# Gram products and attention scores that alternate between the two heads of a pair

## The chip, the cores and the metric

One core of one Trainium2 chip runs the whole program. The metric is the device time of one execution in microseconds (us); less is better. The core has five engines with queues of their own: PE (TensorE, matrix products into PSUM), DVE (VectorE), ACT (ScalarE), POOL (GpSimd) and SP (SyncE, which here issues most transfers). PEld stands for PE's loads of the stationary operand.

## The reference, cut to what matters

Two layers run over 512 tokens (256 of context, then 256 of a latent grid) with 1024 channels. Each layer has a mixer and a gated MLP. The mixer has three branches: a bidirectional RWKV-7 recurrence, a gated linear recurrence and a neighbourhood attention, the first and the last with 16 heads of 64 channels. The change concerns two places. In the recurrence, whose step is

```
sa = jnp.einsum('bhvk,bhk->bhv', S, -kk_t)
S = (S * w_t[:, :, None, :] + sa[..., None] * (kk_t * a_t)[:, :, None, :]
     + v_t[..., None] * k_t[:, :, None, :])
return S, jnp.einsum('bhvk,bhk->bhv', S, r_t)
```

the kernel works by chunks of 64 tokens and needs, for each chunk, head and direction, the products of all keys with all decayed queries of the chunk (the Gram products). In the attention it needs the scores

```
s_loc = jnp.einsum('bhnqd,bhnkd->bhnqk', qb, kb).astype(jnp.float32) * scale + bias.astype(jnp.float32)
s_ctx = jnp.einsum('bhnqd,bhld->bhnql', qpb, k_ctx).astype(jnp.float32) * scale
prob = jax.nn.softmax(jnp.concatenate([s_loc, s_ctx], axis=-1), axis=-1).astype(v.dtype)
```

and, in layer 0 alone, plain attention among the context tokens. Layer 1 puts out latent tokens only.

## The kernel before, in words

Channels lie on the 128 partitions, tokens on the free axis. A channel tile of 128 is a pair of heads: head 0 on partitions 0 to 63, head 1 on 64 to 127. A layer's mixers (`mixers`) loop over 8 pairs. For each pair a string of letters (`order` in `CFG`) says in which order its parts are traced: `1` and `2` prepare a pair for the recurrence (`rw_key`, `rw_prep`), `g` is `rw_gram`, `v` `rw_rows`, `i` and `I` the inverse of the chunks' triangular systems (`rw_inv`, 31 dependent steps on DVE at lines 664 and 666, and `rw_inv2`), `T` the recurrence over the 8 chunks (`rw_seq`), `X`, `Y`, `a`, `b`, `S` the linear recurrence, `Q`, `A` and `P` the attention, `G` and `N` the merge gates. Most of PE's time goes to the projections: `proj` calls `mm3` (lines 246 to 248), which multiplies weights in two parts (`wh`, `wl`) with activations in two parts. `wload` makes these parts: a transfer on SP's queue, `wh` on ACT (line 225), `wl` on DVE or POOL (line 228).

The order on each engine is fixed when the program is built. A list scheduler takes, whenever an engine is free in its forecast, the instruction of highest priority whose operands, and whose place in a tile pool, it expects to be ready. `tc.high_priority(offset=...)` raises priorities (`pri` in `CFG`: 1200 for `g` in layer 0, 20000 in layer 1), and `tc.issue_after(mark)` keeps the attention's PE work behind certain products of the projections: `attn_stages` returns a list of stages, and `sp` in `CFG` gives for each the share of the pair's projections that must have gone before. On the chip each engine then keeps to this order.

`rw_gram` (line 571) goes over direction `d`, head `h`, and half `cg` of the 8 chunks. Each such step takes a PSUM bank of pool `pq`, fills it with four products (line 585; stationary 64 rows by 128 columns, moving 128 columns, or 64 where `nx` is 1, which is layer 1's context half), and empties it: DVE masks one part into `G` (line 587), ACT copies the other where `nx` is 2 (line 590). Pool `pq` has 2 banks, which `rw_rows`, `rw_inv2` and `rw_seq` use too. A product in fp32 shows as two LDWEIGHTS and two MATMUL in the trace, so that a pair has 64 instructions at line 585 in 8 banks.

`attn_s` (line 1001) makes the scores of one head: for each half `x` of 128 queries it takes a bank of pool `pc` (2 banks as well, shared with the linear recurrence's gates, the transposes and others), fills it with two local products (line 1034, 64 rows by 64 columns, one for each block of 64 queries) and one against the context (line 1037, 64 rows by 128 columns; 1043 among context tokens), lets DVE add the bias (line 1039), and hands both banks to `softmax` (lines 897 to 908, which ends with the values in SBUF). `attn_t` transposes these probabilities on PE, again by halves of the queries, each half through a bank of `pc` (line 1054), and ACT copies them to `PT` (line 1055). The stages of a group of tokens are scores of head 0, transposes of head 0, scores of head 1, transposes of head 1, and then `attn_o`, the product with the values for both heads.

Of the kernel before, what the change touches and what calls it, by code (L numbers as in the profile page):

```python
# [10 lines left out]
F32 = mybir.dt.float32  # L11
F32R = mybir.dt.float32r
AF = mybir.ActivationFunctionType
# [38 lines left out]
# per layer: the order in which a head pair's parts are traced, their priorities, how the products of the other  # L52
# mixers are spread beside them, and which engine takes the work that several could take
# [104 lines left out]
class Net:  # L158
# [51 lines left out]
    # ---- weights: raw -> (hi, lo) in float32r  # L210
    def phase(self, l, name, wps=None):
        """From here on the weights rotate among wps; where their low parts are worked out: 1 for GpSimd."""
        self.lo, self.wn = CFG[l]["lo"][name], 0
        if wps:
            self.wps, self.wi = wps, 0
# [49 lines left out]
    # ---- rms statistics of the tokens a ... b - 1: acc holds the sums of squares over the channel tiles  # L265
# [15 lines left out]
    def stat(self, st, sq, a, b, first, last):  # L281
        """Adds the sums of sq over its channels to st, a column for 128 tokens."""
        for T in range(a // P, b // P):
            self.nc.tensor.matmul(st[:, T:T + 1], lhsT=sq[:, T * P:(T + 1) * P], rhs=self.c["one"][:, 0:1],
                                  start=first and T == a // P, stop=last, skip_group_check=True)
# [10 lines left out]
    # ---- conditioning vectors of a layer: mod[128, 48, 2]  # L296
# [16 lines left out]
    def ada_chunk(self, l, n, kind="c"):  # L313
        """Columns 512 n ... 512 n + 511 of the modulation, four column groups side by side on TensorE."""
# [22 lines left out]
        # modulation: h = x rstd (ng (1 + sc)) + sh ; x += (g ng) o rstd  # L337
# [12 lines left out]
    def layer_consts(self, l):  # L350
# [19 lines left out]
        # softplus(-lam) = max(-lam, 0) + log1p(exp(-|lam|)); log1p(u) = 2 atanh(u / (2 + u))  # L370
# [53 lines left out]
    # ---- A: RWKV-7  # L424
# [16 lines left out]
    def rw_start(self, Q):  # L441
# [4 lines left out]
        # stacked over the partitions: (hi, lo) of w, (lo, hi) of a  # L446
# [14 lines left out]
    def rw_key(self, R, Q, p, n0):  # L461
# [15 lines left out]
        # normalised key  # L477
# [93 lines left out]
    def rw_gram(self, R, u, n0):  # L571
        nc = self.nc
        KR, BK = u["KR"], u["BK"]
        G = R.tile([P, 2, 2, 2, NCH, 64], F32, tag="Gm", name="Gm")  # part, d, h, c
        u["Gm"] = G
        gm = self.c["gmask"].rearrange("p (d x t) -> p d x t", d=2, x=2)
        for d in range(2):
            for h in range(2):
                hs = slice(64 * h, 64 * h + 64)
                for cg in range(2):  # L580
                    nx = 2 if 256 * cg >= n0 else 1
                    ps = self.ps("q", "gram").rearrange("p (c x t) -> p c x t", c=4, x=2)
                    for i in range(4):
                        c = 4 * cg + i
                        nc.tensor.matmul(ps[:, i, 0:nx], lhsT=BK[hs, d, c, :], rhs=KR[hs, 0:nx, d, c, :],  # L585
                                         start=True, stop=True)
                    nc.vector.tensor_tensor(G[:, 0, d, h, 4 * cg:4 * cg + 4, :], ps[:, :, 0],
# [9 lines left out]
    def rw_rows(self, R, u, n0):  # L597
# [3 lines left out]
        # from here on [beta; k] decayed to the end of its chunk  # L601
# [3 lines left out]
        # value rows by token, for both directions  # L605
# [12 lines left out]
        # rows by token of [beta; k]  # L618
# [13 lines left out]
    def rw_inv(self, R, u):  # L632
# [9 lines left out]
        if self.cfg['f1']:  # L642
            # the block beside them makes room for the rows of keys
# [10 lines left out]
        # columns s of the inverse: rows 0-63 hold the odd ones, rows 64-127 the even ones, both in the even places  # L654
# [16 lines left out]
    def rw_inv2(self, R, u):  # L671
# [4 lines left out]
        T1 = Ap  # rows 0-31: T11, rows 96-127: Q  # L676
# [134 lines left out]
    # ---- B: RG-LRU  # L811
# [16 lines left out]
    def lru_gates(self, B, u, d):  # L828
# [4 lines left out]
        if self.cfg['lq']:  # L833
            # the parts of the products lie where the second direction's values come
# [54 lines left out]
    # ---- C: neighbourhood attention  # L889
    def softmax(self, C, ps, nk):  # L890
        """ps: list of PSUM views [128, nk] (same width); returns normalised probabilities in SBUF."""
# [22 lines left out]
    def attn_qkv(self, C, p, n0):  # L914
# [13 lines left out]
        # values: 4 windows of 4 rows by 32 columns, then the context  # L928
# [8 lines left out]
    def attn_pre(self, C, u, n0):  # L937
        nc = self.nc
        q, k, vw = u["q"], u["k"], u["vw"]
        # queries by blocks (n, r, c): rotated, then plain  # L940
# [8 lines left out]
        if self.cfg['sq']:  # L949
            # (hi, lo) of a head's plain queries over the partitions, the high parts in the head's own half; the  # L950
            # high parts of the context's keys in both halves, the low ones beside each other
# [24 lines left out]
        # value rows by token: 4 windows, then 2 context tiles  # L976
# [9 lines left out]
    def attn_stages(self, C, u, n0):  # L986
        """The products of the attention in an order in which each finds its operands ready when
        other products stand between."""
        st = []
        for lat in (True, False)[:2 - n0 // 256]:  # L990
            w = [{}, {}]
            for h in range(2):
                st += [[lambda h=h, lat=lat, w=w: self.attn_s(C, u, w[h], h, lat)],
                       [lambda h=h, lat=lat, w=w: self.attn_t(C, u, w[h], h, lat)]]
            st += [[lambda lat=lat, w=w: self.attn_o(C, u, w, lat)]]
# [4 lines left out]
    def attn_s(self, C, u, w, h, lat):  # L1000
        nc = self.nc
        q, k, qb, b4 = u["q"], u["k"], u["qb"], u["b4"]
        hs = slice(64 * h, 64 * h + 64)
        views = []
        if self.cfg['sq']:
            pss = [self.ps("c", f"s{x}") for x in range(2)]
            a, b = (128, 256) if lat else (0, 0)
            for x in range(2):
                cs = slice(b + x * P, b + (x + 1) * P)
                nc.tensor.matmul(pss[x][:, a:a + 256], lhsT=u["QS"][h][:, cs], rhs=u["KD"][:, h], start=True, stop=False,  # L1010
                                 skip_group_check=True)
            for x in range(2):
                cs = slice(b + x * P, b + (x + 1) * P)
                nc.tensor.matmul(pss[x][:, a:a + 256], lhsT=u["QS"][h][hs, cs], rhs=u["KL"][hs], start=False, stop=True,
                                 skip_group_check=True)
            if lat:
                k4 = k[:, 256:].rearrange("p (r c) -> p r c", c=64)
                for x in range(2):
                    for bl in range(2):
                        n = 2 * x + bl  # L1020
                        nc.tensor.matmul(pss[x][64 * bl:64 * bl + 64, 0:128].rearrange("p (r c) -> p r c", c=32),
                                         lhsT=qb[hs, n * 64:n * 64 + 64], rhs=k4[hs, :, self.KW[n]:self.KW[n] + 32],
                                         start=True, stop=True, skip_group_check=True)
                    nc.vector.scalar_tensor_tensor(pss[x][:, 0:128], b4[:, h, x], 8.0, pss[x][:, 0:128],
                                                   op0=ALU.mult, op1=ALU.add)
            w["pr"] = self.softmax(C, [t[:, 0:384 if lat else 256] for t in pss], 384 if lat else 256)
            return
        for x in range(2):
            ps = self.ps("c", f"s{x}")
            if lat:  # L1030
                k4 = k[:, 256:].rearrange("p (r c) -> p r c", c=64)
                for bl in range(2):
                    n = 2 * x + bl
# [561 lines left out]
```

## Time and profile before

| | us |
|---|---|
| median of 3 runs | 3056.64 |
| lowest and highest run | 3052.81, 3072.35 |
| span of the profiled execution | 3050.6 |
| PE busy in it | 2886.2 (95%) |
| DVE busy in it | 1968.9 (65%) |
| ACT busy in it | 1411.1 (46%) |
| POOL busy in it | 840.6 (28%) |

The span runs from the first to the last instruction of one execution. A run's time also has what lies around the span: 2.2 us for the lowest run, 6.0 us for the median, if they were like the profiled one. The mixers of layer 0 take about the stretch from 80 to 1130 us, those of layer 1 from 1860 to 2720 us; the change touches nothing outside. PE's ends are modelled, so a busy PE isn't PE at its peak, and the busy time of a group of instructions reaches a little past the start of what follows.

### The profile page before, as it was taken

The numbers are of one execution on the slowest core, as the hardware profiler recorded it, in microseconds if no ns is written. First come the engines' busy times: TensorE is split into PE (matmuls) and PEld (weight loads), VectorE is DVE, ScalarE is ACT, GpSimd is POOL, SyncE is SP. The second block draws the span as 40 slices with busy tenths as digits, with TensorE's granted clock in tenths as the row PEclk, the third lists the DMA queues.
The fourth block names the chain that finished last, engine by engine and source line by source line (L and its number), as shares of the span: only waits on it lengthen the run. The fifth ranks groups of instructions, "written<-read, shape, count | busy, mean of one in ns | idle before, by whom it ended". The sixth has DMA issues, their size and how long they took to land. (4 is left out here: it accounts for less than half of the span.)

```text
span 3050.6 us, 53179 instructions
## 1 busy us (share of the span) xinstructions
PE 2886.2 (95%) x21104; PEld 2265.9 (74%) x21104; DVE 1968.9 (65%) x3745; ACT 1411.1 (46%) x2485; POOL 840.6 (28%) x788
## 2 busy tenths in 40 slices
PE   7999999999999999999999998998999999998998
PEld 5666776766767678687778886776776777788898
DVE  6757658576686653465444267788677778775784
ACT  4454455554455452253323245454554545554553
POOL 3341322424234225100000113433432433414220
PEclk9999999999999899998999998998988999999899
DMA  6222122211222225755562352222222122245653
GB/s 229 81 70 67 59 71 66 74 60 56 69 76 70 84 100 180 273 190 180 198 223 92 107 183 82 62 78 69 68 72 69 62 70 78 77 140 205 222 188 115
DMA packets 130553, 344.39 MB, mean 113 GB/s; under 512 B 14720, under 2 KB 41600, under 8 KB 130304
## 3 DMA queue, kind: packets, MB, share of 16 engines
q1 hardware_dynamic: 123392, 334.69, 33.1%
q10 hardware_dynamic: 6912, 6.29, 0.7%
q8 instruction: 166, 2.72, 0.4%
q14 instruction: 83, 0.68, 0.1%
HBM read 301.08 MB, written 25.17 MB: 107 GB/s over the span
## 5 line engine op out<-in xcount | busy, mean ns | idle before, releaser
L225 ACT ACTIVATE wh<-wr 128x1024 fp32r<-128x1024 f32 (+1 forms) x402 | 420.8, 1048 | 581.0 <-PE pj L247 209.1
L248 PE MATMUL pj<-hh,wl 128*128 128x512 f32 (+1 forms) x1440 | 559.0, 389 | 41.4 <-DVE wl L228 40.0
L246 PE MATMUL pj<-hh,wh 128*128 128x512 f32 (+1 forms) x1440 | 569.7, 397 | 5.8 <-ACT gt L1088 3.0
L228 DVE TENSOR_TENSOR wl<-wr,wh 128x1024 fp32r<-128x1024 f32 (+1 forms) x310 | 398.2, 1285 | 266.5 <-ACT wh L225 244.2
L247 PE MATMUL pj<-hl,wh 128*128 128x512 f32 (+1 forms) x1440 | 556.0, 386 | 0.0
L228 POOL TENSOR_TENSOR wl<-wr,wh 128x1024 fp32r<-128x1024 f32 (+1 forms) x92 | 221.1, 2403 | 637.1 <-ACT wh L225 343.6
L248 PEld LDWEIGHTS pj<-hh,wl 128*128 128x128 f32 x1440 | 280.7, 195 | 104.6 <-DVE wl L228 45.7
L246 PEld LDWEIGHTS pj<-hh,wh 128*128 128x128 f32 x1440 | 280.6, 195 | 70.0 <-issue 16.4
L247 PEld LDWEIGHTS pj<-hl,wh 128*128 128x128 f32 x1440 | 280.4, 195 | 55.1 <-issue 13.4
L666 DVE TENSOR_TENSOR AT<-AT,itmp 128x126 f32<-128x126 f32 (+22 forms) x496 | 154.7, 312 | 11.8
L732 POOL TENSOR_TENSOR r<-SV,gC 64x256 f32<-64x256 f32 x96 | 84.2, 877 | 242.0 <-DVE SV L745 139.8
L664 DVE TENSOR_TENSOR itmp<-AT 128x126 f32<-128x126 f32 (+22 forms) x496 | 138.1, 278 | 12.0
L585 PEld LDWEIGHTS gram<-KR,BK 64*128 64x128 f32 x1024 | 116.3, 193 | 27.4 <-ACT Gm L590 14.8
L585 PE MATMUL gram<-KR,BK 64*128 64x128 f32 (+1 forms) x1024 | 131.3, 288 | 4.9 <-ACT Gm L590 4.7
L246 PE MATMUL fo<-fh,wh 128*128 128x256 f32 (+1 forms) x418 | 131.0, 313 | 0.0
L248 PE MATMUL fo<-fh,wl 128*128 128x256 f32 (+1 forms) x418 | 130.7, 313 | 0.0
L247 PE MATMUL fo<-fl,wh 128*128 128x256 f32 (+1 forms) x418 | 130.4, 312 | 0.0
L246 PE MATMUL fu<-hh,wh 128*128 128x256 f32 (+1 forms) x384 | 126.2, 330 | 3.1 <-DVE fgs L1347 2.4
L246 PE MATMUL fg<-hh,wh 128*128 128x256 f32 (+1 forms) x384 | 127.2, 333 | 0.1
L248 PE MATMUL fu<-hh,wl 128*128 128x256 f32 (+1 forms) x384 | 126.4, 330 | 0.8 <-DVE wl L228 0.8
L247 PE MATMUL fg<-hl,wh 128*128 128x256 f32 (+1 forms) x384 | 126.0, 330 | 0.0
L247 PE MATMUL fu<-hl,wh 128*128 128x256 f32 (+1 forms) x384 | 125.8, 328 | 0.0
(344 smaller groups left out, 6481.6 us busy)
## 6 DMA issues: line engine op xcount, KB each, us to landing
wr<-in_w_in SPq DMA_DIRECT2D x180, 512.0 KB, 3.2
aw<-in_ada_w SPq DMA_DIRECT2D x96, 512.0 KB, 4.4
wr<-in_ffn_w_in SPq DMA_DIRECT2D x96, 512.0 KB, 3.4
wr<-in_w_branch SPq DMA_DIRECT2D x48, 512.0 KB, 3.3
wr<-in_ffn_w_out SPq DMA_DIRECT2D x36, 512.0 KB, 3.5
wr<-in_w_out SPq DMA_DIRECT2D x24, 512.0 KB, 4.4
Gm<-KR SPq DMA_DIRECT2D x32, 256.0 KB, 3.6
wr<-in_ffn_w_out SPq DMA_DIRECT2D x18, 384.0 KB, 3.1
```

The lines of the kernel that those rows point to most:

```text
L225: nc.scalar.activation(hi, raw, AF.Copy)
L228: eng.tensor_tensor(lo, raw, hi.bitcast(F32), op=ALU.subtract)
L246: nc.tensor.matmul(o, lhsT=a, rhs=xh[k][:, n0:n1], start=(first and k == 0), stop=False)
L247: nc.tensor.matmul(o, lhsT=a, rhs=xl[k][:, n0:n1], start=False, stop=False)
L248: m = nc.tensor.matmul(o, lhsT=b, rhs=xh[k][:, n0:n1], start=False, stop=(last and k == kt - 1))
L585: nc.tensor.matmul(ps[:, i, 0:nx], lhsT=BK[hs, d, c, :], rhs=KR[hs, 0:nx, d, c, :], start=True, stop=True)
L664: eng.tensor_tensor(tmp, Ap[:, q + 1:32, q:q + 1].to_broadcast([P, nt, ns]), Tf[:, q:q + 1, 0:2 * ns:2].to_broadcast([P, nt, ns]), op=ALU. ...
L666: eng.tensor_tensor(Tf[:, q + 1:32, 0:2 * ns:2], Tf[:, q + 1:32, 0:2 * ns:2], tmp, op=ALU.subtract)
L732: nc.gpsimd.tensor_tensor(sg, S0, gcb, op=ALU.mult)
```

## The change

Three things change; the rest of the diff takes out comments and a branch of `attn_s` that no layer uses (`sq` is 0 in both).

- In `rw_gram` the loops run over `d`, then `cg`, and both heads' banks are taken together. The products alternate between the heads: chunk 0 of head 0 into one bank, chunk 0 of head 1 into the other, and so on. The two banks are emptied behind the eight products, head 0's first.
- `attn_s` takes a half `x` of the queries in place of a head `h`. It takes a bank for each head and alternates: local products of block 0 for both heads, of block 1 for both, then the context's for both. The bias is added for both behind all products, and `softmax` gets the two heads' banks.
- `attn_t` follows: at a stage it transposes the two heads' probabilities of one half of the queries; both `PT` tiles are taken at the first half. The list of stages has the same length and the same shares `sp`.

The numbers of products, additions, copies and transfers, their shapes and their operands are the same as before.

```diff
         for d in range(2):
-            for h in range(2):
-                hs = slice(64 * h, 64 * h + 64)
-                for cg in range(2):
-                    nx = 2 if 256 * cg >= n0 else 1
-                    ps = self.ps("q", "gram").rearrange("p (c x t) -> p c x t", c=4, x=2)
-                    for i in range(4):
-                        c = 4 * cg + i
-                        nc.tensor.matmul(ps[:, i, 0:nx], lhsT=BK[hs, d, c, :], rhs=KR[hs, 0:nx, d, c, :],
+            for cg in range(2):
+                nx = 2 if 256 * cg >= n0 else 1
+                pss = [self.ps("q", "gram").rearrange("p (c x t) -> p c x t", c=4, x=2) for h in range(2)]
+                for i in range(4):
+                    c = 4 * cg + i
+                    for h in range(2):
+                        hs = slice(64 * h, 64 * h + 64)
+                        nc.tensor.matmul(pss[h][:, i, 0:nx], lhsT=BK[hs, d, c, :], rhs=KR[hs, 0:nx, d, c, :],
                                          start=True, stop=True)
+                for h, ps in enumerate(pss):
                     nc.vector.tensor_tensor(G[:, 0, d, h, 4 * cg:4 * cg + 4, :], ps[:, :, 0],
                                             gm[:, d:d + 1, 0].to_broadcast([P, 4, 64]), op=ALU.mult)
...
-            for h in range(2):
-                st += [[lambda h=h, lat=lat, w=w: self.attn_s(C, u, w[h], h, lat)],
-                       [lambda h=h, lat=lat, w=w: self.attn_t(C, u, w[h], h, lat)]]
+            for x in range(2):
+                st += [[lambda x=x, lat=lat, w=w: self.attn_s(C, u, w, x, lat)],
+                       [lambda x=x, lat=lat, w=w: self.attn_t(C, u, w, x, lat)]]
...
+        hs = [slice(0, 64), slice(64, 128)]
+        pss = [self.ps("c", f"s{h}") for h in range(2)]
+        if lat:
+            k4 = k[:, 256:].rearrange("p (r c) -> p r c", c=64)
+            for bl in range(2):
+                n = 2 * x + bl
+                for h in range(2):
+                    nc.tensor.matmul(pss[h][64 * bl:64 * bl + 64, 0:128].rearrange("p (r c) -> p r c", c=32),
+                                     lhsT=qb[hs[h], n * 64:n * 64 + 64], rhs=k4[hs[h], :, self.KW[n]:self.KW[n] + 32],
                                      start=True, stop=True, skip_group_check=True)
...
+        o = 128 if lat else 0
+        src, a = (qb, 256) if lat else (q, 0)
+        for h in range(2):
+            nc.tensor.matmul(pss[h][:, o:o + 256], lhsT=src[hs[h], a + x * P:a + (x + 1) * P], rhs=k[hs[h], 0:256],
+                             start=True, stop=True, skip_group_check=True)
+        if lat:
+            for h in range(2):
+                nc.vector.scalar_tensor_tensor(pss[h][:, 0:128], b4[:, h, x], 8.0, pss[h][:, 0:128],
                                                op0=ALU.mult, op1=ALU.add)
...
+        w[x]["pr"] = self.softmax(C, [ps[:, 0:o + 256] for ps in pss], o + 256)
...
-        PT = w["PT"] = C.tile([P, 3, 256], F32, tag=("f1", "av")[h], name="PT")
-        for x in range(2):
+        if x == 0:
+            for h in range(2):
+                w[h]["PT"] = C.tile([P, 3, 256], F32, tag=("f1", "av")[h], name="PT")
+        for h in range(2):
             pt = self.ps("c", "pt")
             for j in range(nj):
-                nc.tensor.transpose(pt[:, j * P:(j + 1) * P], w["pr"][x][:, j * P:(j + 1) * P], self.ident)
+                nc.tensor.transpose(pt[:, j * P:(j + 1) * P], w[x]["pr"][h][:, j * P:(j + 1) * P], self.ident)
```

## Rows read from the trace of the kernel before

**Rows 1.** The page's first line.

```profile
span 3050.6 us, 53179 instructions
```

**Rows 2.** Busy time by stretch: from:to us, its length, each engine busy (instructions), clock, DMA.

```profile
80.00:1130.00 1050.00, 1014.83 (x7136) 725.57 (x7137) 694.38 (x1474) 508.76 (x955) 323.33 (x323) 0.97 0.22 70
1860.00:2720.00 860.00, 805.39 (x6315) 620.48 (x6317) 666.01 (x1322) 447.13 (x821) 311.42 (x327) 0.94 0.23 74
```

**Rows 3.** PE's waits, layer 0's mixers, then layer 1's: total us, times, longest.

```profile
PE gram L585 <- ACT Gm L590: 4.7, 6, 1.5
...
PE pj L248 <- DVE wl L228: 40.0, 9, 7.4
```

**Rows 4.** The chain that ended last, in layer 1's mixers, shares of 1860 to 2720 us.

```profile
by line: DVE AT L666 9.5%; PE pj L246 8.3%; PE pj L248 8.3%; PE pj L247 8.0%; DVE itmp L664 7.8%; PE gram L585 5.6%; issue 5.2%; PE r L720 3.8%; PE sa L735 3.6%; DVE wl L228 2.8%; PE sp L741 2.6%; DVE G L522 2.4%; PE Q L691 2.2%; PE Q L685 
```

**Rows 5.** Timeline, PE: start us, us, instructions; 16 of one head among projections (layer 0).

```profile
81.62 0.39 PE L246 MATMUL pj<-hh,wh 128*128 128x512 f32 x1
81.85 0.40 PE L247 MATMUL pj<-hl,wh 128*128 128x512 f32 x1
82.18 2.05 PE L585 MATMUL gram<-KR,BK 64*128 64x128 f32 x16
84.16 0.50 PE L248 MATMUL pj<-hh,wl 128*128 128x512 f32 x1
84.49 0.39 PE L246 MATMUL pj<-hh,wh 128*128 128x512 f32 x1
```

**Rows 6.** Timeline, PE: 16 that change heads halfway (layer 0), and 8 of one head.

```profile
218.83 1.71 PE L585 MATMUL gram<-KR,BK 64*128 64x128 f32 x16
...
2305.83 1.10 PE L585 MATMUL gram<-KR,BK 64*128 64x64 f32 x8
...
2314.78 1.16 PE L585 MATMUL gram<-KR,BK 64*128 64x128 f32 x8
```

**Rows 7.** Timeline, PE: scores of head 1 and Gram products of head 0 (layer 1).

```profile
1974.33 0.48 PE L1037 MATMUL s<-k,qb 64*128 64x256 f32 x1
1974.33 0.54 PE L585 MATMUL gram<-KR,BK 64*128 64x64 f32 x3
```

**Rows 8.** Busy time by stretch (as rows 2, without POOL) of instructions on the tile gram.

```profile
80.00:1130.00 1050.00, 69.50 (x512) 60.75 (x512) 26.01 (x64) 23.70 (x64) 0.97 0.22 70
...
1860.00:2720.00 860.00, 61.75 (x512) 55.54 (x512) 26.58 (x64) 12.18 (x32) 0.94 0.23 74
```

**Rows 9.** What empties a bank: line, engine, out<-in, shapes, count | busy, mean ns.

```profile
L587 DVE TENSOR_TENSOR Gm<-gram,cst 128x256 f32<-128x256 f32 x128 | 52.6, 418 | 27.9 <-PE gram L585 26.1
...
L590 ACT ACTIVATE Gm<-gram 128x256 f32<-128x256 f32 x96 | 35.9, 380 | 79.0 <-DVE Gm L587 78.5
```

**Rows 10.** Timeline, PE: the scores of one head, both halves of the queries back to back.

```profile
1097.62 0.43 PE L1034 MATMUL s<-k,qb 64*64 64x128 f32 x4
1097.98 0.70 PE L1037 MATMUL s<-k,qb 64*128 64x256 f32 x2
1098.61 0.44 PE L1034 MATMUL s<-k,qb 64*64 64x128 f32 x4
```

**Rows 11.** Timeline, PE: the second head's scores, its halves apart (layer 1).

```profile
2519.61 0.44 PE L1034 MATMUL s<-k,qb 64*64 64x128 f32 x4
...
2520.60 0.44 PE L1054 MATMUL pt<-cst,pr 128*128 128x128 f32 x2
...
2521.67 0.43 PE L1034 MATMUL s<-k,qb 64*64 64x128 f32 x4
```

**Rows 12.** Timeline, PE: context scores, the two halves (layer 0).

```profile
249.44 0.70 PE L1043 MATMUL s<-k,q 64*128 64x256 f32 x2
250.07 0.50 PE L248 MATMUL pj<-hh,wl 128*128 128x512 f32 x1
250.50 0.70 PE L1043 MATMUL s<-k,q 64*128 64x256 f32 x2
```

**Rows 13.** Timeline, DVE: what can stand before a bank's emptying in its queue (layer 1).

```profile
2312.12 1.86 DVE L228 TENSOR_TENSOR wl<-wr,wh 128x1024 fp32r<-128x1024 f32 x1 [0.23 <-PE pj L248]
```

More of the change, by code (lines that the diff above doesn't have):

```diff
@@ L998, in attn_stages, with attn_s @@
         return st
-    def attn_s(self, C, u, w, h, lat):
+    def attn_s(self, C, u, w, x, lat):
         nc = self.nc
         q, k, qb, b4 = u["q"], u["k"], u["qb"], u["b4"]
[L1003 to L1007, printed above, removed]
-            for x in range(2):
[L1009 to L1033, printed above, removed]
-                    nc.tensor.matmul(ps[64 * bl:64 * bl + 64, 0:128].rearrange("p (r c) -> p r c", c=32),
-                                     lhsT=qb[hs, n * 64:n * 64 + 64], rhs=k4[hs, :, self.KW[n]:self.KW[n] + 32],
-                                     start=True, stop=True, skip_group_check=True)
-                nc.tensor.matmul(ps[:, 128:384], lhsT=qb[hs, 256 + x * P:256 + (x + 1) * P], rhs=k[hs, 0:256],
-                                 start=True, stop=True, skip_group_check=True)
-                nc.vector.scalar_tensor_tensor(ps[:, 0:128], b4[:, h, x], 8.0, ps[:, 0:128],
-                                               op0=ALU.mult, op1=ALU.add)
-                views.append(ps[:, 0:384])
-            else:
-                nc.tensor.matmul(ps[:, 0:256], lhsT=q[hs, x * P:(x + 1) * P], rhs=k[hs, 0:256], start=True, stop=True)
-                views.append(ps[:, 0:256])
-        w["pr"] = self.softmax(C, views, 384 if lat else 256)
@@ L1047, in attn_t @@
-    def attn_t(self, C, u, w, h, lat):
+        hs = [slice(0, 64), slice(64, 128)]
[7 more added lines that the diff above has]
+                                     lhsT=qb[hs[h], n * 64:n * 64 + 64], rhs=k4[hs[h], :, self.KW[n]:self.KW[n] + 32],
+                                     start=True, stop=True, skip_group_check=True)
@@ L1048, in attn_t @@
+        w[x]["pr"] = self.softmax(C, [ps[:, 0:o + 256] for ps in pss], o + 256)
+    def attn_t(self, C, u, w, x, lat):
         nc = self.nc
         nj = 3 if lat else 2
-        PT = w["PT"] = C.tile([P, 3, 256], F32, tag=("f1", "av")[h], name="PT")
-        for x in range(2):
+        if x == 0:
+            for h in range(2):
+                w[h]["PT"] = C.tile([P, 3, 256], F32, tag=("f1", "av")[h], name="PT")
+        for h in range(2):
             pt = self.ps("c", "pt")
             for j in range(nj):
-                nc.tensor.transpose(pt[:, j * P:(j + 1) * P], w["pr"][x][:, j * P:(j + 1) * P], self.ident)
-            nc.scalar.activation(PT[:, 0:nj, x * P:(x + 1) * P], pt[:, 0:nj * P].rearrange("p (j q) -> p j q", j=nj), AF.Copy)
+                nc.tensor.transpose(pt[:, j * P:(j + 1) * P], w[x]["pr"][h][:, j * P:(j + 1) * P], self.ident)
+            nc.scalar.activation(w[h]["PT"][:, 0:nj, x * P:(x + 1) * P], pt[:, 0:nj * P].rearrange("p (j q) -> p j q", j=nj), AF.Copy)
```

## The prediction

> **What bounds the kernel now.** I read the busy time by stretch first. In layer 0's mixers PE is busy 1015 of 1050 us, no other engine more than 726 [rows 2]: PE's queue sets the time, and what PE no longer spends is nearly all saved. In layer 1's PE has 805 of 860 us [rows 2], and of its 55 idle us 40 go to projections that wait for a `wl` part behind DVE's own work [rows 3]. There PE and a chain of dependencies end close together, so I read the chain next: DVE's inverse (lines 664 and 666) holds 17% of the stretch, and Gram products hold 5.6%, 48 us of the 62 that they are busy there [rows 4, 8]. So the Gram products of layer 1 lie mostly on the path itself. Their banks cost PE little in layer 0 today: 4.7 us of waits for ACT's copy [rows 3].
>
> **What PE does with a Gram burst.** Sixteen instructions of one head (two banks) take 2.05 us [rows 5]. Sixteen whose second half is the other head take 1.71, and eight take 1.16 [rows 6]. So where heads change, the second head's products start while the first head's still run. The plainest row is in layer 1, where head 1's score product and head 0's first Gram products start in the same hundredth of a microsecond [rows 7]: products whose operands lie on different halves of the partitions, with different banks, run side by side, loads included. If the pair alternates from the first product on, sixteen should take what eight of one head take, 1.16 us. Nothing in the trace runs alternately for a whole burst, so that figure is carried over from the neighbouring rows.
>
> **The Gram products, summed.** They are 1024 instructions, 64 groups of 16 under the new loop (8 pairs, 2 layers, 2 directions, 2 halves of the chunks). Now they are busy 69.5 us in layer 0 and 61.75 in layer 1, 131.3 together [rows 8]. Fully alternating: 64 x 1.16 = 74.2, a saving of 57. That needs both banks free when a group begins. They are for a pair's first group. Later groups find them freed one after the other, since one DVE queue masks both: head 1's bank is later by about one eviction, 0.42 us [rows 9]. The scheduler issues what is ready, so head 0 goes ahead alone for that time. So 16 first groups at 1.16 and 48 at 1.16 + 0.42 = 1.58 make 94.4, a saving of 37: 22 in layer 0 (69.5 - 47.2) and 15 in layer 1 (61.75 - 47.2). The bounds: if the second bank always comes a whole head later, a group is like today's changing burst, 1.71, in all 109 and a saving of 22; at the other end 57. I take 37, because the eviction's own length is the only lag that must be there.
>
> [...]
>
> **The scores, summed.** One head's half of the queries takes PE 0.99 us (1097.62 to 1098.61), two in a row 1.98 [rows 10]. The products of two heads lie on different halves of the operands' partitions; if they run side by side as in rows 7, a stage of both heads takes one such time: 0.99 saved per stage where both banks are free at its start. A first stage (`x` = 0) comes behind projections, long after the banks' last use: 16 of them, 16 us, half in each layer. A second stage comes behind the transposes of the first, whose banks ACT frees one by one; today the second head's two halves lie 2.06 us apart, a transpose between them [rows 11]. Then head 0's three products go first and head 1's later, and nothing is shared: I count a quarter of 16, 4 us (bounds 0 and 16). The context scores in layer 0 lie 1.06 us apart with a projection between [rows 12] for the same reason; 1 us (bounds 0 and 10: 16 stages of 0.63). Together 21: 11 in layer 0, 10 in layer 1.
>
> **Fewer changes of shape.** A visit by products of another shape costs the projections: starts go from 0.23 us apart to 0.33 at the entry and 0.33 behind the exit [rows 5], 0.2 a visit. Layer 1's Gram products come in five visits a pair today, from the eight at 2305.83 to the eight at 2314.78 [rows 6], and would come in four; each first score stage loses one. 24 visits x 0.2 = 5 us, 2 in layer 0 and 3 in layer 1 (bounds 0 and 10).
>
> **What costs nothing, and what covers it.** DVE's and ACT's work has the same count and shapes. The bias addition and `softmax` of head 0 now start behind head 1's products, up to 0.63 us later (1097.98 to 1098.61 [rows 10]), covered by the projections that stand between scores and transposes. `PT` of head 1 is taken one stage pair earlier; its place holds the values' windows, which PE has transposed in `A`, before any stage. No transfer moves, so SP's and POOL's queues are as before.
>
> **The sum.** Layer 0: 22 + 11 + 2 = 35; by PE's share there, 97%, 34. Layer 1: 15 + 10 + 3 = 28; by the Gram products' share on the chain, 48 of 62, 22. The profiled span of 3050.6 [rows 1] becomes 2994.6. The runs stand 2.2 (lowest) to 6.0 us (median) above that span; with 4 of it, **2999 us**, 1.9% under the median of 3056.6.
>
> **Rivals.**
>
> *Full alternation.* Both banks come together and all stages share: 57 + 42 + 10 = 109 us of PE time. Rows 7 speak for it, the single DVE queue against it. At 90% realised, 2957 us. Chance 0.17.
>
> *Alternation in the source only.* The scheduler sees the heads' banks become free apart and puts out four products of one head, then four of the other. Then Gram groups take 1.71 (saving 22), first stages a half (8): 30 us of PE time, 26 realised, about 3029 us. Today's order speaks for it, since the halves of a stage lie apart [rows 11, 12]; against it, Gram products have a high priority and their evictions follow closely. Chance 0.18.
>
> *Layer 1 keeps its time.* If DVE's inverse and evictions set layer 1's pace, only layer 0's 34 us come: 3021 us. For it speaks DVE's part of the chain, against it the 48 us of Gram products on it [rows 4]. Chance 0.13.
>
> *The bank wait takes the place of the products (slower).* A group can no longer fill one bank while the other is emptied: its last eviction must end before the next group's head 1 can begin, and PE keeps its order, so everything queued behind that LDWEIGHTS, projections included, waits too. Back to back that is two DVE evictions and one ACT copy, 0.42 + 0.42 + 0.38 = 1.2 us [rows 9], for 48 later groups 59 us, which would eat the whole gain of 56. A `wl` of 1.86 us ahead of the eviction in DVE's queue [rows 13] would make it 3.1 us a group. It decides from 1.2 us a group on; at 2.0, 96 us of waits, the time is 3095. [...] The trace so far bears it out little: PE waited 4.7 us in all for these banks [rows 3], because the scheduler puts projections between. Chance 0.12, of which 0.05 within 1%.
>
> **Chances and range.** The forecast, between 2975 and 3020, has 0.40. Faster by over 1% (below 3026; 1% is about what a measurement of this kernel can tell from no change): forecast 0.40, full 0.17, layer 1 unchanged 0.13, and 0.04 of the source-only case: 0.74. Within 1%: 0.14 and 0.05: 0.19. Slower by over 1%: 0.07. The range reaches from 2945 (a little under full alternation) to 3060 (the bank wait at its balance); outside are some 0.07 below and 0.10 above.
>
> **What would show it.** Right: Gram bursts of 16 that take 1.2 to 1.6 us, starts of the two heads a few ns apart; PE's busy time on `gram` at 90 to 100 us in place of 131; one block of local scores for two heads in each first stage, two in each second. Wrong: bursts of 1.7 us or more (source-only), a wait "gram <- DVE or ACT Gm" of tens of us (the bank wait), or layer 1's stretch unchanged while PE's idle time in it grows. What would make it wrong without touching these steps: a schedule that falls differently for the inverse or the recurrence, since every priority and share was set with the old order of these products.

## The result, and the profile after

The changed kernel takes 3100.5 us (median of four runs, 3092.9 to 3117.9); the kernel before took 3056.6 beside it. The ratio is 1.013, 95% interval 1.009 to 1.017: slower by 44 us, where I had forecast 58 us faster. The profiled execution answers to [rows 1]:

```profile
span 3091.1 us, 53143 instructions
```

Busy time by stretch (columns as in [rows 2]; the last three are the granted clock, the DMA share and GB/s). So that the stretches hold the same work, each runs from a layer's first product on `pj` to the first on `pbr`, the projection behind the mixers; layer 0 and layer 1 of the kernel before, then of the changed one:

```profile
33.94:1136.54 1102.60, 1063.93 (x7336) 763.03 (x7337) 730.32 (x1547) 535.26 (x997) 350.04 (x344) 0.97 0.22 72
1792.55:2691.38 898.83, 837.48 (x6426) 650.00 (x6425) 688.27 (x1340) 465.08 (x839) 322.34 (x338) 0.94 0.24 78
...
33.41:1147.54 1114.13, 1064.73 (x7337) 759.48 (x7337) 718.94 (x1546) 532.39 (x997) 352.22 (x344) 0.95 0.23 71
1799.37:2730.67 931.30, 861.76 (x6442) 674.78 (x6440) 680.12 (x1342) 462.29 (x843) 318.24 (x338) 0.90 0.24 75
```

The engines have the work they had before. Both layers got longer: layer 0 by 11.5 us, where I had 34 less, layer 1 by 32.5, where I had 22 less. What fell is the granted clock: 0.97 to 0.95 in layer 0, 0.94 to 0.90 in layer 1. Of the instructions on the tile gram alone (as [rows 8], without POOL), in stretches that hold all of them:

```profile
80.00:1125.00 1045.00, 55.25 (x512) 47.32 (x512) 24.08 (x64) 22.26 (x64) 0.95 0.22 69
1865.00:2770.00 905.00, 70.63 (x512) 62.52 (x512) 25.75 (x64) 12.31 (x32) 0.89 0.23 71
```

In layer 0 they fell from 69.5 to 55.3 us; in layer 1 they rose from 61.75 to 70.6. PE's waits over the whole span (as [rows 3]):

```profile
PE pj L248 <- DVE wl L228: 36.3, 8, 4.8
PE r L722 <- DVE SV L747: 15.1, 7, 2.2
PE yt L793 <- DVE cen L780: 14.7, 7, 3.7
...
PE Q L687 <- DVE AT L680: 11.3, 8, 1.9
...
PE pb L567 <- DVE ks L565: 8.7, 2, 6.1
...
PE gram L586 <- ACT Gm L592: 7.5, 7, 1.7
```

The wait for the banks went from 4.7 to 7.5 us: that rival isn't it. PE's idle time in all, span less busy time, rose from 164 to 183 us: the waits at `yt`, `r`, `Q` and `pb` grew and others shrank. In the timeline of PE, a first Gram group of layer 0, then the local scores of two heads:

```profile
81.56 1.16 PE L586 MATMUL gram<-KR,BK 64*128 64x128 f32 x16
...
212.66 0.45 PE L1013 MATMUL s<-k,qb 64*64 64x128 f32 x8
```

Sixteen alternating products take 1.16 us, the figure of the forecast, and eight local products the time of four [rows 10]. But most groups don't look like this. One pair of layer 1, from the recurrence's last step:

```profile
2306.42 1.11 PE L722 MATMUL r<-SV,Gm 128*64 128x64 f32 x8 [2.16 <-DVE SV L747]
...
2321.33 1.10 PE L586 MATMUL gram<-KR,BK 64*128 64x64 f32 x8
...
2324.00 4.55 PE L586 MATMUL gram<-KR,BK 64*128 64x64 f32 x24
...
2330.49 2.45 PE L586 MATMUL gram<-KR,BK 64*128 64x64 f32 x16
...
2334.45 2.09 PE L586 MATMUL gram<-KR,BK 64*128 64x128 f32 x16
```

Eight of head 0 alone, then 24 in a row, head 1's eight first: the scheduler put four products of one head, then four of the other. The pair's last sixteen do alternate, and take 2.09 us in place of 1.16. Over the whole trace 226 of 512 pairs of Gram products start within 30 ns of each other (39 before); of the 64 groups 13 start in such pairs from end to end. And the 24 take 4.55 us where the granted clock is 0.50. The same pair by stretches (columns as in [rows 2]):

```profile
2280.00:2303.00 23.00, 23.00 (x221) 17.21 (x221) 11.88 (x21) 11.90 (x23) 11.27 (x12) 1.00 0.17 53
2303.00:2317.00 14.00, 11.84 (x62) 8.51 (x59) 9.72 (x21) 5.34 (x12) 6.30 (x11) 0.63 0.20 57
2317.00:2324.00 7.00, 7.00 (x45) 5.12 (x43) 4.28 (x9) 3.05 (x5) 0.94 (x2) 0.96 0.06 20
2324.00:2337.00 13.00, 13.00 (x74) 11.77 (x74) 7.11 (x17) 3.22 (x8) 5.93 (x4) 0.50 0.24 72
```

The clock records of the two profiled executions hold two values, 1.00 and 0.50. In the kernel before, a 128x512 product starts 427 ns behind another of its shape where the clock is 0.50, 231 ns where it is 1.00 (medians). A clock of 0.50 is called half clock here. The expectations write 1.2 GHz for it, which is 512 columns in 427 ns with one column taken as a cycle, an estimate. Two stretches of each pair run at half clock: one from the recurrence's end, behind PE's wait of 2.16 us, and one in the Gram stage, in which PE is busy for all of its 13 us. The kernel before, in the same two places (the recurrence's end, the Gram stage):

```profile
2290.00:2297.00 7.00, 7.00 (x40) 5.02 (x40) 3.05 (x8) 1.01 (x2) 0.64 (x2) 0.54 0.00 0
2297.00:2306.00 9.00, 9.00 (x64) 5.79 (x62) 5.18 (x18) 4.96 (x13) 2.79 (x4) 1.00 0.15 33
2306.00:2317.00 11.00, 10.95 (x100) 8.87 (x100) 8.22 (x17) 4.42 (x10) 6.45 (x6) 1.00 0.24 82
```

Averaged over seven pairs of layer 1, the way from the recurrence's end to the first Gram product has 9.8 us at half clock (1.5 before) and the Gram stage some 9 (0 before).

### The profile page after: what moved, and what is told of

The parts are those of the page before. It is cut to its first block, busy times and chain, and to the rows that moved or that the text cites. A ratio compares the mean times of both kernels' runs of the same rounds, so it can differ in the third digit from the quotient of the medians.

```text
span 3091.1 us, 53143 instructions
## 1 busy us (share of the span) xinstructions
PE 2907.9 (94%) x21104; PEld 2283.7 (74%) x21104; DVE 1949.1 (63%) x3745; ACT 1404.1 (45%) x2485; POOL 838.7 (27%) x788
## 5 line engine op out<-in xcount | busy, mean ns | idle before, releaser
L228 DVE TENSOR_TENSOR wl<-wr,wh 128x1024 fp32r<-128x1024 f32 (+1 forms) x310 | 404.8, 1306 | 319.1 <-ACT wh L225 308.5
L248 PE MATMUL pj<-hh,wl 128*128 128x512 f32 (+1 forms) x1440 | 570.7, 397 | 37.5 <-DVE wl L228 36.3
L247 PE MATMUL pj<-hl,wh 128*128 128x512 f32 (+1 forms) x1440 | 568.8, 395 | 0.0
L248 PEld LDWEIGHTS pj<-hh,wl 128*128 128x128 f32 x1440 | 287.6, 200 | 98.8 <-DVE wl L228 39.5
L246 PEld LDWEIGHTS pj<-hh,wh 128*128 128x128 f32 x1440 | 286.8, 200 | 76.2 <-issue 19.6
L247 PEld LDWEIGHTS pj<-hl,wh 128*128 128x128 f32 x1440 | 286.9, 199 | 53.6 <-issue 7.6
L734 POOL TENSOR_TENSOR r<-SV,gC 64x256 f32<-64x256 f32 x96 | 94.5, 985 | 328.1 <-DVE SV L747 175.0
L666 DVE TENSOR_TENSOR itmp<-AT 128x126 f32<-128x126 f32 (+22 forms) x496 | 130.9, 264 | 11.1
L586 PEld LDWEIGHTS gram<-KR,BK 64*128 64x128 f32 x1024 | 109.8, 233 | 27.8 <-ACT Gm L592 17.3
L248 PE MATMUL fg<-hh,wl 128*128 128x256 f32 (+1 forms) x384 | 125.5, 328 | 0.0
```

What stands on the lines that cost most here:

```text
L228: eng.tensor_tensor(lo, raw, hi.bitcast(F32), op=ALU.subtract)
L246: nc.tensor.matmul(o, lhsT=a, rhs=xh[k][:, n0:n1], start=(first and k == 0), stop=False)
L247: nc.tensor.matmul(o, lhsT=a, rhs=xl[k][:, n0:n1], start=False, stop=False)
L248: m = nc.tensor.matmul(o, lhsT=b, rhs=xh[k][:, n0:n1], start=False, stop=(last and k == kt - 1))
L586: nc.tensor.matmul(pss[h][:, i, 0:nx], lhsT=BK[hs, d, c, :], rhs=KR[hs, 0:nx, d, c, :], start=True, stop=True)
L666: eng.tensor_tensor(tmp, Ap[:, q + 1:32, q:q + 1].to_broadcast([P, nt, ns]), Tf[:, q:q + 1, 0:2 * ns:2].to_broadcast([P, nt, ns]), op=ALU. ...
```

## The experiments

All runs in one table. "At half clock" is 2 x (1 - mean granted clock) x span, the median over the runs. Runs of one and the same kernel differ in that time, and it goes with most of their difference: all 86 runs of the kernel before, 3051 to 3082 us at clocks of 0.964 to 0.950, have a correlation of 0.90 with it. A straight line gives 0.33 us per us at half clock for before and 0.31 to 0.45 for the eight other kernels with ten runs or more (the changed kernel's own four runs give 0.64). So the last column takes 0.4 of it off each run's time, an estimate from these lines; there the runs of a kernel agree with a standard deviation of some 3 us (4.6 in the changed kernel, 5.2 in the one with the wait filled). The ratio is to runs of before beside each kernel, whose medians lie between 3056.6 and 3063.5 us; a difference of two rows of the table can carry these few us.

| kernel | median us | ratio to before | at half clock | less 0.4 of it |
|---|---|---|---|---|
| before (all runs) | 3059.1 | | 248 | 2959 |
| changed | 3100.5 | 1.0131 (1.0090 to 1.0172) | 387 | 2946 |
| Gram part alone | 3069.2 | 1.0032 (1.0013 to 1.0052) | 276 | 2960 |
| attention part alone | 3079.2 | 1.0068 (1.0046 to 1.0090) | 289 | 2966 |
| Gram by halves, heads not alternating | 3062.6 | 1.0001 (0.9981 to 1.0021) | 254 | 2961 |
| attention by halves, not alternating | 3066.2 | 1.0014 (0.9994 to 1.0034) | 273 | 2959 |
| Gram part, alternation forced | 3084.6 | 1.0081 (1.0050 to 1.0112) | 284 | 2976 |
| changed, one half of the rows | 3171.6 | 1.0356 (1.0320 to 1.0392) | 475 | 2985 |
| before, one half of the rows | 3081.7 | 1.0090 (1.0057 to 1.0124) | 283 | 2968 |
| changed, all rows | 3085.3 | 1.0052 (1.0015 to 1.0088) | 296 | 2965 |
| before, all rows | 3034.8 | 0.9921 (0.9897 to 0.9945) | 209 | 2950 |
| Gram part, yt late | 3062.3 | 1.0013 (0.9996 to 1.0030) | 269 | 2954 |
| before, yt late | 3074.7 | 1.0049 (1.0028 to 1.0069) | 267 | 2966 |
| changed, wait filled | 3150.5 | 1.0307 (1.0261 to 1.0352) | 412 | 2988 |
| before, wait filled | 3085.8 | 1.0081 (1.0057 to 1.0105) | 271 | 2978 |
| Gram part in layer 0 alone, yt late | 3048.2 | 0.9972 (0.9951 to 0.9993) | 262 | 2944 |

**Which part.** The Gram part alone: `rw_gram` of the change, the rest of before. The attention part alone: the reverse.

> Only rw_gram is taken from the changed kernel; attention is that of before. Three theories of the 44 us lost. Theory G (the Gram part carries the loss): in the changed kernel's trace each pair of layer 1 has a stretch at 1.2 GHz within its Gram stage and another at the recurrence's end that before had not, and the way from the recurrence's end to the next Gram product is 14 us in place of 9; then this kernel takes 3085 to 3105 us and its granted clock is 0.94 to 0.95. Theory S (the attention part carries it, by its transposes, whose start-to-next time rose from 29.5 to 48.5 us): this kernel takes about what the Gram products save, 3030 to 3050. Theory B (each half alone is harmless, the two orders collide): 3040 to 3060.

> Only the attention is taken from the changed kernel (stages of 128 queries of both heads, scores alternating); rw_gram is that of before. Theory G: 3035 to 3060 us, the granted clock that of before, 0.96. Theory S: 3080 to 3105. Theory B: 3040 to 3060.

Neither part carries the loss alone: 0.3% and 0.7%, together 1.0 of the 1.3%. Each is a loss although its products got shorter (Gram products 131 to 106 us, scores 105 to 82). Of the three theories none had both parts losing.

**Same order, no head beside the other.** Two kernels with every instruction in its place on every engine; only the rows of head 0 are read for both heads:

```diff
-                        hs = slice(64 * h, 64 * h + 64)
+                        hs = slice(0, 64)
```

> The changed kernel with its instructions and their order on every engine as they are, but all Gram products and all scores read head 0's half of the partitions for both heads, so that two neighbours can't run side by side (head 1's part of both results is computed from head 0's channels; nothing else changes). Theory C (clock): the products that run side by side leave the engine less to do, the clock is granted at 1.2 GHz for 373 us in place of 251, and the projections pay; without side-by-side running the clock comes back to 0.96 and the time to 3055 to 3075 us. Theory O (order): the place of the products in the program order makes the loss, and what runs side by side is a small gain already had; this kernel then takes 3100 to 3130 us, the Gram products' 122 us going up to 130 to 145, and the clock stays at 0.93 to 0.95.

> The kernel before, its instructions and their order on every engine untouched, but all Gram products and all scores read head 0's half of the partitions for both heads (head 1's part of both is computed from head 0's channels; nothing else changes). The changed kernel lost 71 us when it was treated in this way (3171.6 in place of 3100.5). If the kernel before shares little (its Gram products take 129.6 us from start to next start, near 64 groups of 2.05), this one takes 3065 to 3085 us; the alternation then is worth some 50 to 65 us, and the new order costs some 90 to 105 with the side-by-side running taken away from both. If the kernel before shares much already, it takes 3115 us or more; the alternation then is worth 15 or less, and the order costs about 55.

The changed kernel loses 71 us by it, the one before 24. So with the order held, two heads side by side are worth 71 us in the changed kernel and 24 before: the alternation brought 47. With that taken from both, the changed order alone costs 90 us (3171.6 to 3081.7). Taken against the runs of before beside each, the four numbers are 67, 24, 43 and 87. (The two blocks of a head's local scores, which write different halves of a bank's partitions, still start together: 70 starts within 30 ns in the kernel before, 70 and 100 in the two on one half. What is gone is one head beside the other: no two Gram products start so.) My theory that side-by-side products lower the clock fell: without it the time at half clock rises, by 88 us in the changed kernel and 35 before.

**Same order, all rows.** The same two kernels with `hs = slice(0, P)`: the products read 128 rows, so again no head runs beside the other (no two Gram products start within 30 ns).

> The changed kernel, instructions and order on every engine untouched, but all Gram products and scores read all 128 partitions of their operands, for both heads (the products then sum over both heads' channels, so the results are others; nothing else changes). No two can run side by side, as in the run that reads one half (3171.6 us, 487 us at 1.2 GHz). Theory C (in the changed order long stretches hold only products of half the rows, the clock falls for that, and it is the clock that costs): cold time falls towards 250 us and the time to 3080 to 3110, a gap of 10 to 35 to the order of before treated in the same way. Theory O (waits and evictions of the new order): 3155 to 3180, the gap of 90 stays.

> The kernel before with the same products on all 128 rows, its order untouched: the other half of the comparison. Reading one half took 3081.7 us with 282 us at 1.2 GHz. Theory C: 3065 to 3080 us, a little colder time less; theory O: 3075 to 3090, 90 us below the changed kernel's.

The gap between the two orders shrinks from 90 to 50 us, between the two theories; neither had the kernel before as fast as 3034.8. Of the 90, the clock takes 0.4 x (475 - 283) = 77, of the 50, 0.4 x (296 - 209) = 35; what is left is 13 and 15, the price of the order without the clock (17 and 15 by the table's last column). It is an estimate and hangs on the factor: with 0.31 it is 30 and 23, with 0.45 it is 4 and 11. The Gram stage of layer 1 shows it directly; with all rows (from the first Gram product to the last):

```profile
2333.00:2345.00 12.00, 11.44 (x94) 10.63 (x93) 10.07 (x20) 3.68 (x10) 6.91 (x5) 1.00 0.28 87
```

and with one half:

```profile
2393.00:2411.00 18.00, 18.00 (x93) 16.14 (x93) 9.62 (x23) 4.10 (x10) 7.05 (x5) 0.64 0.20 61
```

With the same instructions in the same order, the clock stays at 1.00 in all seven pairs when the products fill the rows. The products themselves are no quicker: at a clock of 1.00 one starts 112 ns behind the other (median) in both of these kernels. The stretches behind the recurrence's end stay, at 7.8 us a pair.

**Is it the alternation or the halves?** In each part the new loops, but head 0's products ahead of head 1's in the source:

```diff
-                for i in range(4):
-                    c = 4 * cg + i
-                    for h in range(2):
+                for h in range(2):
+                    for i in range(4):
+                        c = 4 * cg + i
```

> Attention of before; rw_gram takes both heads' banks together as in the changed kernel, but its source gives head 0's four products, then head 1's four. Theory A (the alternation of the source is what the Gram part brings): Gram products as in before, 125 to 130 us from start to next start, and 10 to 20 us slower than the Gram part alone, 3078 to 3090. Theory S (the list scheduler lays the heads out four and four anyway): within 5 us of it, 3064 to 3074, with nearly the same bursts.

> rw_gram of before; attention by halves of the queries as in the changed kernel, but within a stage all products of head 0 go before those of head 1 in the source. The attention part alone costs 21 us (ratio 1.0068), although its scores are busy 82 us in place of 105. Theory O (the stages by halves, which change what the transposes and the softmax wait for, cost it): the scores lose their 23 us of side-by-side running and the time is 3080 to 3100 us. Theory A (the alternation itself costs, by letting the clock fall): back to 3055 to 3068.

Both are level with before. In the second, every engine's instructions come in the order of before, name by name (but for products that start within 10 ns of each other). In the first, theory A had the products right (132 us busy, as before) and the time wrong; theory S had neither. In the second theory A holds: the scores are busy 107 us, and four of seven pairs of layer 1 take what they took before to 0.1 us. So the halves cost nothing; the first kernel's order in layer 1 is not that of before either, and its time is. What moves the order so that it costs is the alternation of the source.

**Alternation forced.** Each Gram product is put behind the other head's by a mark.

```diff
+                        with (self.tc.issue_after(m.ins) if m is not None else ExitStack()):
```

> Attention of before; rw_gram of the changed kernel, with each product put behind the other head's in PE's order by an explicit mark, so that the heads alternate there (in the changed kernel most groups were laid out as four of one head, then four of the other). Theory A (the change lost because the alternation did not reach the program order): Gram bursts of 16 take 1.1 us, the products' start-to-next time falls from 129.6 us to 75 to 90, and the time is 3000 to 3030 us. Theory O (what counts is where the groups stand in the order): the products get as short, but the time stays within 3050 to 3110. Theory C (side-by-side running lowers the clock): more side-by-side running, more time at 1.2 GHz, over 3100.

Theory O. The products are busy 102 us in place of 131 and the clock is that of before in the profiled execution (0.960), yet the time is 0.8% up: in that execution PE idles 203 us of its span of 3077.5, 38 more than before.

**Where a shorter Gram stage goes.** Layer 0 of the Gram part alone, PE:

```profile
613.14 1.16 PE L586 MATMUL gram<-KR,BK 64*128 64x128 f32 x16
614.23 0.44 PE L1056 MATMUL pt<-cst,pr 128*128 128x128 f32 x2
618.14 0.46 PE L793 MATMUL yt<-cst,cen 128*128 128x128 f32 x2 [3.47 <-DVE cen L780]
```

PE's products are done earlier; the next thing in its order is `yt`, which needs `cen` from DVE. In total PE waits 23.9 us for it, 8.5 before. Next, layer 0's `yt` is put behind the transposes `bt`, by their place in the source (`v` ahead of `O`) and by a mark, here and, as a control, in the kernel before:

```diff
-  'order': 'gioOvIX|aQY||bGSA12TNB|P',
+  'order': 'giovOIX|aQY||bGSA12TNB|P',
...
+                            if n0 == 0:
+                                z.enter_context(tc.issue_after(self.btm.ins))
                             self.rw_out2(R, u if done else ul, n0)
```

> The Gram part alone (3069 us) lost its gain of layer 0, 23 us of Gram products, to one wait: PE stands 3.7 us before the transposes yt in six pairs until DVE has made cen (23.9 us in all, 8.5 in before). Here layer 0's yt comes behind the transposes bt in PE's order, by an explicit mark; all else is that kernel. Theory W (the gain went into this wait): the wait falls under 5 us and the time to 3045 to 3058. Theory N (PE's wait is only the place where a chain shows, and another wait takes over): 3060 to 3075, with the same idle time under another name.

> The kernel before with the same move of yt behind bt, as the control. Theory W: 8.5 us of that wait to gain at most, 3048 to 3062, so that the Gram part is worth a gain or nothing once the wait is out of both. Theory O (any move of the order costs, since shares and priorities fit the old one): 3065 to 3085 without a single product changed.

That wait goes to about nothing, and another appears:

```profile
PE vt L616 <- ACT Gm L592: 11.3, 4, 2.9
```

The time falls by 7 us (by 4 against the runs of before beside each, and the two intervals overlap), not by 11 to 24: theory N more than W. The control loses 0.5%, as theory O has it: an order that suits one kernel costs in the other. With `yt` late in both, the Gram part is a gain of 12 us (3074.7 to 3062.3).

**The wait at the recurrence's end.** Eight products that nobody reads go into the wait before the last `r` in layer 1:

```diff
+            if n0 and i == NCH - 1:
+                with self.tc.issue_after(lsp.ins):
+                    for _ in range(8):
+                        nc.tensor.matmul(pr, lhsT=self.hh[0][:, 0:P], rhs=self.hh[1], start=True, stop=True)
```

> The changed kernel; in layer 1, ahead of each pair's last step of the recurrence, where PE stands 2.6 us before r, eight products of 128x512 that nobody reads are put into that wait (some 1.9 us, into r's own bank). Nothing the kernel computes is left out. Theory W (the clock falls for 10.2 us at each recurrence's end since PE stands still there): those stretches at 1.2 GHz go, layer 1's cold time falls from 195 us by 50 to 70, and the time to 3065 to 3085 us in spite of the added products. Theory N (the clock falls for the narrow products behind, whatever PE does in the wait): the stretches stay or move into the Gram stage, and the time stays at 3095 to 3115.

> The kernel before with the same eight products in the same place, as the control: it has 1.5 us a pair at 1.2 GHz at the recurrence's end, so there is little to gain, and the products don't quite fit into its wait of 1.7 to 2.0 us. Theory W: 3052 to 3065 us. Theory N, or if moving the order costs by itself: 3065 to 3090.

In the changed kernel the wait falls to

```profile
PE r L727 <- DVE SV L752: 5.4, 6, 1.1
```

and the stretch behind it from 9.8 to 2.8 us a pair at half clock. But the time rises by 50 us: the rest of layer 1's order moved too, and the slow stretches came up in the recurrence (9.4 us a pair in place of 1.0, on average) and before it (13.7 in place of 5.7). So theory W holds for the place and fails for the time. The control loses 27 us against the runs beside it, as theory N has it. Its way from the recurrence's end to the first Gram product has nothing left at half clock, and from layer 1's first Gram product to the last pair's its profiled execution takes 767.1 us in place of 771.8; what that loses lies behind, from the last pair's first Gram product to the end of the span (441.5 us in place of 417.5). So a part of the 50 may be what the fill costs in any order.

**A version that beats both.** Alternating Gram products in layer 0 alone, with `yt` late; layer 1's order on PE is that of before.

> The alternating Gram products in layer 0 alone, where PE sets the time, with yt behind bt there; layer 1 and the attention are those of before (layer 1's order on PE is the same as before, instruction for instruction). By the traces of its two halves: layer 0 from its first Gram product to its last recurrence 1009 us (before 1014), layer 1 866 as before. Theory O (each gain holds where the order is left alone): 3048 to 3056 us, a little under before. Theory C (the clock moves freely between pairs and kernels, so no such sum holds): anywhere from 3055 to 3075.

3048.2 us, 0.28% under before (0.07 to 0.49%). Its Gram products in layer 0 take 54.5 us (before 69.5). The expectation of 3048 to 3056 was added up from two layers measured apart.

## Why the prediction was wrong, point by point

**What PE does with a burst: right at a clock of 1.00.** 1.16 us for sixteen that alternate, in the group at 81.56 us with the two heads' starts 6 to 7 ns apart; at half clock sixteen take 2.09. The loads ran side by side too: where [rows 7] were read, those of lines 1037 and 585 start at 1974.32 and 1974.33 us, 0.18 us each.

**The Gram saving: too large.** I had the products at 94 us, 47.2 in each layer; measured are 126, 55.3 and 70.6. The step that failed is "1.16 + 0.42": it lets only the eviction's lag keep the heads apart. The scheduler, in whose forecast the heads' banks come free apart, laid out four and four, as the source-only rival said. In seven pairs of layer 1 three of the four groups came so, and there the products also ran at half clock and got longer than before.

**The scores: about right.** Busy time on the scores fell from 105 to 90 us; I had 21. Second stages share nothing, as said.

**"What costs nothing": the step that failed most.** I argued that DVE's and ACT's work is the same in count and shape and priced the order at nothing. By the estimates above it costs 13 to 17 us beside the clock (PE's waits at `yt`, `r`, `Q` and `pb` together rose from 28.9 to 49.8 us, its idle time in all by 19) and, through the clock, 0.4 x (387 - 248) = 56 us. I had named a schedule that falls differently as what could undo the forecast, and had given it neither a price nor a chance.

**97% realised: wrong in kind.** PE's share does bound layer 0, but PE's time isn't made of fixed durations: in layer 0 the Gram products' busy time fell by 14 us, and PE's rose from 1063.9 to 1064.7. [Rows 2] had the clock, 0.97 and 0.94, as a column that I didn't use.

**The balance.** Less 0.4 of the time at half clock, the changed kernel is 14 us faster than before, a third of what the terms promise when 13 to 15 us go to the order; the clock takes 56 back, and 42 of loss remain, beside 44 measured. That the two meet is no proof, since the 14 and the 56 rest on the same factor; with 0.31 or 0.45 the clock's part is 43 or 63 us. The 4 us that I put around the span are 1.8 in nearly every run that gives both.

**The rivals.** The bank wait gave nearly the measured time, 3095, by chance: it needs 96 us of waits, and PE waited 7.5. What came was another order, with the clock as most of its price.

**What stays open.** In the Gram stage the runs of half-row products go with the fall of the clock: in the pair shown it is 0.64 on one half of the rows and 1.00 on all. For the stretch behind the recurrence's end, in layer 1, no such single cause is shown: filling the wait removes it there and it comes back elsewhere. How much of the loss is the clock and how much the order's waits rests on the factor of 0.4.

## What to carry to other kernels

A shorter run of products paid here only where the order around it and the granted clock held: in layer 1 of the whole change the clock fell from 0.94 to 0.90, and the Gram products took 70.6 us in place of 61.75. So read the clock column by stage before summing PE time, and compare kernels with the time at half clock taken into account. To tell order from mechanism, keep every instruction in its place and change only what it reads. Where a list scheduler is tuned to an order, change one layer or one part at a time: here the Gram part, in layer 0 alone and with `yt` late, gained 0.3%, and the whole change lost 1.3%.

## What the runs showed of the hardware

**The clock and the rows.** Letting the Gram products and scores read 128 rows in place of 64 made the kernel before 0.8% faster (3034.8 us), although no head runs beside the other any more: 209 us at half clock in place of 248. The changed kernel's Gram stage shown above, in which the trace counts PE as busy from end to end (13.00 of 13.00 us), ran at 0.50, and of two kernels with one order the one with products on half of the rows ran it at 0.64, the one on all rows at 1.00.

**Half of the rows among all rows.** The clock isn't the whole of that gain; 0.4 x 39 us are 16 of the 24. With the clock at 1.00 throughout, one context score between two products of a projection took 953 ns from the start of the one to the start of the other, in the kernel before and in its run on one half, and 516 ns when it read all rows (medians of 15 visits each); sixteen Gram instructions of one head took 2302 ns on one half and 1963 on all rows (4 visits each). So a visit on half of the rows took 0.3 to 0.4 us more. Both orders gain about the same beside the clock, 20 and 18 us in the table's last column (2985 to 2965, 2968 to 2950), so it isn't what brought the gap between them from 90 to 50.

**DVE behind POOL.** The multiplication `cen <- cen,lr` (128x512) took 2.38 us in seven of eight pairs of the Gram part alone, in four of the changed kernel and in two of the kernel before. DVE's line and POOL's:

```profile
615.71 2.38 DVE L780 TENSOR_TENSOR cen<-cen,lr 128x512 f32<-128x512 f32 x1 [1.22 <-POOL lr L779]
```

```profile
615.64 1.89 POOL L606 TENSOR_TENSOR BK<-BK,gE 128x1024 f32<-128x1024 f32 x1
```

In a pair of the changed kernel, DVE's and POOL's:

```profile
492.24 0.69 DVE L780 TENSOR_TENSOR cen<-cen,lr 128x512 f32<-128x512 f32 x1 [1.78 <-POOL lr L779]
```

```profile
492.83 1.90 POOL L606 TENSOR_TENSOR BK<-BK,gE 128x1024 f32<-128x1024 f32 x1 [0.62 <-PE gram L586]
```

Where POOL's product started 0.07 us ahead, DVE's took 1.69 us more, and where DVE started first, 0.69. POOL's product waits for the Gram products' last read of `BK` (20 times in the changed kernel, 75.0 us of idle time in all), so Gram products that end earlier move it, and 1.7 us of the wait at `yt` came from there. POOL's product shows nothing of the kind: in the second pair it started 0.10 us before DVE's ended and took 1.90 us, and all 32 of the changed kernel took 1.89 to 1.90.
